# Moving work off GpSimd beside the row gather of a hybrid mLSTM/GLA/PEER block

## The chip, the cores and the metric

The kernel runs on one core of one Trainium2 chip. It has five instruction streams: TensorE (PE, with its weight loads PEld), VectorE (DVE), ScalarE (ACT), GpSimd (POOL) and SyncE (SP, which here only issues DMAs). Each stream runs in its own order, and waits for the others by semaphores. The metric is the time of one execution in microseconds (us). Three runs of the kernel before took 3162.22, 3174.01 and 3175.31 us, so the median is 3174.01 us. The profiled execution took 3167.59 us; its span, from the first to the last instruction, is 3165.8 us, which leaves 1.8 us around it.

## The reference

The layer has two halves. The first, a token mixer with two recurrent head groups, ends before the part that changes here. The second half is PEER, a sparse feed-forward layer with 16,384 experts; each expert is one row u and one row v of 1024 numbers. Per token and head, 16 experts of 16,384 are chosen, and with 8 heads that makes 128 experts for each of the 1024 tokens:

```python
def peer_ffn(h, wq, keys, u_tab, v_tab):
    def retrieve(xb):                               # 128 tokens at a time
        q = (xb @ wq).reshape(PEER_BLOCK, PEER_HEADS, 2, PEER_QDIM // 2)
        s = jnp.einsum('tphq,phkq->tphk', q, keys)
        top_s, top_i = lax.top_k(s, PEER_TOPK)
        ...                                         # best 16 of the 256 pairs: idx, and scores best_s
        g = jax.nn.softmax(best_s.astype(jnp.float32), axis=-1).astype(xb.dtype)
        act = jax.nn.gelu(jnp.einsum('tpkd,td->tpk', u_tab[idx], xb), approximate=False)
        return jnp.einsum('tpk,tpkd->td', g * act, v_tab[idx])
```

So a token's output is the sum over its 128 experts of g * gelu(u . h) * v, in float32.

## The kernel before

The 1024 tokens are eight blocks of 128. Three of them (set A) are computed by gathering, five (set B, 640 tokens) densely.

**The gather.** `gather_all` is a Python generator of some 398 steps, 128 for each block of set A. In step i the queue of GpSimd fetches the u and v rows of one expert per token, 128 rows of 8 KB, into a tile `uv` [128 x 2 x 1024] (L936; four such tiles, and step i fetches for step i + 2). The dot product u . h is one instruction that multiplies and sums (L983 on VectorE). `gate` makes gelu and the factor g on ScalarE (L948, L949), and `add` adds act * v to the block's sum on VectorE (L961). Until the dense stage that sum lies in PSUM (`accP`), afterwards in SBUF (`acc`); `settle` copies it over. While `share[0]` is 2, during query stage B, every other dot product is split: GpSimd multiplies (L981) and ScalarE sums (L947).

**The dense part.** For set B the scores of all 128 x 128 experts are computed: `u_side` multiplies the h of set B by a chunk of 128 u rows (`ua`, 48 matmuls, L1017). Each float32 operand is split into a high and a low part, so that three cheaper products replace one. The high part of u is made on ScalarE (`uh`, L1042), the low part `ul` (L1043) before the dense stage on GpSimd and in it on VectorE. The first 84 chunks are done early (`early_all`), beside the work on queries, and stored in DRAM; the other 44 come in the dense stage, in which the chunks are multiplied by v (`po`, L1405).

**The stages.** Query stage A finds the experts of set A. From 870 us on the gather and the early chunks run beside: selection A (870 to 985 us), query stage B (985 to 1150: projections `pq`, top-16 searches on VectorE, splits `qlo` of the query weights on GpSimd, L1122), selection B (1150 to 1367), and the table loop (1367 to 1829), which builds the gates of set B. One of its 80 iterations makes four one-hot tiles on VectorE (L1294 to L1297, o, oh, ol and oh again) and 16 small matmuls `gb` (L1275, L1276), whose results ScalarE copies out (L1278). What is left of the early chunks follows (1829 to 1866; here called the tail), and then the dense stage to the end.

**What sets the order.** The instructions of every engine stand as the Python code emits them. `ticks` advances the gather by a fixed rate per microsecond of modelled work. `fill` advances the early chunks by quarters (12 matmuls, 1.6 us in its account) as long as the modelled clock of TensorE is behind that of VectorE plus 6 us. When the table loop ends, the quarters that are left are emitted in a row, with 0.2 gather steps per modelled us. The one-hot tiles of the loop have two buffers each, and the `gb` matmuls of an iteration are emitted one iteration later.

## Time and profile before

| what | value |
|---|---|
| median of three runs | 3174.01 us |
| profiled execution | 3167.59 us |
| its span | 3165.8 us |
| mean granted TensorE clock | 0.952 |
| PE, PEld, DVE, ACT, POOL busy over the span | 91%, 81%, 80%, 41%, 31% |
| data moved | 831.44 MB, mean 263 GB/s |

The clock is a share of 2.4 GHz: in a stretch at 1.0 TensorE had its full clock, at 0.5 it had 1.2 GHz. A view of stretches has, for each engine, its busy time in us in that stretch and the number of its instructions, then the granted clock, the mean busy share of the 16 DMA engines and the rate they moved data at. A float32 matmul stands in the trace as two records. A row on one line of the code has the least, the median and the largest duration in ns. A row on waits says who waited for whom, the sum in us, how often, and the longest.

### The profile page before, as it was taken

To read this page: it belongs to the slowest core of one execution; us is meant where nothing else is said; L and a number is where in the kernel's file an instruction comes from. 1 tells how busy PE (TensorE), PEld (TensorE's weight loads), DVE (VectorE), ACT (ScalarE), POOL (GpSimd) and SP (SyncE) were. 2 spreads that over 40 slices of the span, in tenths; PEclk is the share of its full clock that TensorE was granted. 3 is DMA by queue.
4 is the path that set the end of the run, shared out by engine and by line. 5 is a ranking of instruction groups with operands and counts; after the bars stand their busy time and mean duration, and the time that the engine had idled before them with its cause. 6 is when DMAs were issued, how large, how long until landed. Compare 5 with 4: busy or idle time off the path is not lost.

```text
span 3165.8 us, 47649 instructions
## 1 busy us (share of the span) xinstructions
PE 2882.2 (91%) x17321; PEld 2555.5 (81%) x17321; DVE 2518.5 (80%) x4809; ACT 1307.1 (41%) x2909; POOL 973.6 (31%) x760
## 2 busy tenths in 40 slices
PE   7999998998998997878898889999998999999997
PEld 3799896776998987878887888888887788888885
DVE  6633318666798999999999958888888788888885
ACT  4622224444443454545555634333333333333332
POOL 1000002323455776654443432222222222222211
PEclk9999999789999998889999999999999999999999
DMA  5155428535367876768898999999999899999983
GB/s 208 58 181 165 132 85 268 169 107 193 108 231 267 287 269 231 248 225 311 322 317 298 335 349 341 346 342 335 338 345 350 308 332 332 341 337 343 343 292 116
DMA packets 374380, 831.44 MB, mean 263 GB/s; under 512 B 27000, under 2 KB 198648, under 8 KB 324736
## 3 DMA queue, kind: packets, MB, share of 16 engines
q0 software_dynamic: 57600, 411.07, 34.9%
q1 hardware_dynamic: 292624, 347.74, 34.4%
q10 hardware_dynamic: 23920, 69.59, 5.6%
q8 instruction: 136, 2.23, 0.3%
q14 instruction: 100, 0.82, 0.1%
HBM read 729.38 MB, written 98.91 MB: 262 GB/s over the span
## 4 chain that ended last, share of the span: by engine, by line
issue 27%; DVE 17%; POOL 8%; PE 4%; DMA 1%; ACT 0%; POOLq 0%; SPq 0%; DVEq 0%
POOL uv L936 8%; DVE ol L1296 4%; PE po L1405 3%; DVE uv L983 3%; DVE accP L961 2%; DVE oh L1297 2%; DVE oh L1295 2%; DVE o L1294 2%; PE ua L1017 2%; DMA vr<-uv 1%; DMA uv<-uv,idx 1%; DVE acc L961 0%; DVE vl L1371 0%; DVE accB L1412 0%; DMA ft<-d_mod 0%
## 5 line engine op out<-in xcount | busy, mean ns | idle before, releaser
L936 POOL DMA_INDIRECT uv<-uv,idx x384 | 454.5, 1184 | 1299.1 <-DVE acc L961 891.5
L1405 PE MATMUL po<-vh,wh 128*128 128x512 f32 x1255 | 498.8, 397 | 49.7 <-DVE accB L1412 45.4
L1017 PE MATMUL ua<-hBhi,uh 128*128 128x320 f32 x2048 | 492.1, 322 | 39.0 <-ACT uh L1042 26.6
L1405 PE MATMUL po<-vl,wh 128*128 128x512 f32 x1255 | 498.4, 397 | 12.1 <-DVE vl L1371 12.0
L1017 PE MATMUL ua<-hBhi,ul 128*128 128x320 f32 x2048 | 482.5, 318 | 22.0 <-POOL ul L1043 21.7
L1405 PE MATMUL po<-vh,wl 128*128 128x512 f32 x1255 | 495.3, 395 | 0.0
L1017 PE MATMUL ua<-hBlo,uh 128*128 128x320 f32 x2048 | 480.9, 317 | 0.0
L983 DVE SCALAR_TENSOR_TENSOR uv<-uv,h2a 128x1024 f32<-128x1024 f32 x351 | 437.4, 1246 | 49.3 <-DMA uv<-uv,idx 48.9
L1017 PEld LDWEIGHTS ua<-hBhi,uh 128*128 128x128 f32 x2048 | 356.1, 196 | 45.9 <-ACT uh L1042 28.8
L1017 PEld LDWEIGHTS ua<-hBhi,ul 128*128 128x128 f32 x2048 | 355.0, 195 | 26.5 <-POOL ul L1043 26.5
L1017 PEld LDWEIGHTS ua<-hBlo,uh 128*128 128x128 f32 x2048 | 356.9, 195 | 0.0
L1405 PEld LDWEIGHTS po<-vh,wh 128*128 128x128 f32 x1255 | 240.0, 191 | 108.7 <-DVE accB L1412 53.4
L961 DVE SCALAR_TENSOR_TENSOR acc<-uv,act,acc 128x1024 f32<-128x1024 f32 x237 | 303.2, 1279 | 0.2 <-ACT act L949 0.2
L1405 PEld LDWEIGHTS po<-vl,wh 128*128 128x128 f32 x1255 | 240.1, 191 | 65.4 <-DVE vl L1371 17.7
L1405 PEld LDWEIGHTS po<-vh,wl 128*128 128x128 f32 x1255 | 240.3, 191 | 50.5
L1043 POOL TENSOR_TENSOR ul<-ur,uh 128x512 fp32r<-128x512 f32 x170 | 236.6, 1415 | 79.8 <-ACT uh L1042 75.5
L1381 ACT ACTIVATE wh<-w 128x640 fp32r<-128x640 f32 x128 | 94.6, 739 | 396.8 <-DVE w L1378 395.2
L1370 ACT ACTIVATE vh<-vr 128x512 fp32r<-128x512 f32 x251 | 156.6, 625 | 161.3 <-PE po L1405 160.9
L948 ACT ACTIVATE act<-act 128x1 f32<-128x1 f32 x384 | 75.9, 198 | 318.5 <-DVE uv L983 316.7
L961 DVE SCALAR_TENSOR_TENSOR accP<-uv,act,accP 128x1024 f32<-128x1024 f32 x144 | 184.6, 1282 | 15.1 <-ACT act L949 15.1
L1371 DVE TENSOR_TENSOR vl<-vr,vh 128x512 fp32r<-128x512 f32 x251 | 170.9, 685 | 25.3 <-ACT vh L1370 24.8
L1278 ACT ACTIVATE gtl<-gb 128x512 f32<-128x512 f32 x160 | 160.3, 1111 | 71.6 <-PE gb L1276 62.8
(376 smaller groups left out, 5668.7 us busy)
## 6 DMA issues: line engine op xcount, KB each, us to landing
ur<-uC SPq DMA_DIRECT2D x256, 256.0 KB, 6.4
vr<-uv SPq DMA_DIRECT2D x256, 256.0 KB, 7.1
d_G<-gtl ACTq DMA_DIRECT2D x80, 512.0 KB, 5.4
gch<-d_G SPq DMA_DIRECT2D x64, 640.0 KB, 9.7
d_A<-w ACTq DMA_DIRECT2D x84, 320.0 KB, 5.3
w<-d_A SPq DMA_DIRECT2D x84, 320.0 KB, 7.6
wm<-w_mod SPq DMA_DIRECT2D x32, 512.0 KB, 3.9
qraw<-wq SPq DMA_DIRECT2D x32, 512.0 KB, 4.3
```

Of the source, the lines that this page charges most:

```text
L936: G.indirect_dma_start(out=t.rearrange("p a d -> p (a d)"), out_offset=None, in_=A["uv"], in_offset=bass.IndirectOffsetOnAxis(ap=idxs[n][: ...
L948: S.activation(acts[i], acts[i], AF.Gelu)
L961: V.scalar_tensor_tensor(acc, v, act, acc, op0=ALU.mult, op1=ALU.add)
L983: V.scalar_tensor_tensor(t, t, 1.0, h2s[n], op0=ALU.mult, op1=ALU.mult, accum_out=acts[i])
L1017: T.matmul(pt[:, :b - a], l[:, kt], m[:, kt, a:b], start=(kt == 0 and wi == 0), stop=(kt == KT - 1 and wi == 2))
L1043: usplit[0].tensor_tensor(ul[:, k], ur, uh[:, k].bitcast(F32), op=ALU.subtract)
L1278: S.activation(gt[:, :, tt:tt + 4].rearrange("p e t -> p t e"), pt.rearrange("p (t e) -> p t e", e=P), AF.Copy, scale=1.0 / 4096.0)
L1296: V.tensor_tensor(ol, oh, pairs(glT, b, t0), op=ALU.mult)
L1370: S.activation(vh, vr[n], AF.Copy)
L1371: V.tensor_tensor(vl, vr.pop(n), vh.bitcast(F32), op=ALU.subtract)
L1381: S.activation(wh, w, AF.Copy)
L1405: T.matmul(po, st[:, b * P:(b + 1) * P], m, start=(start and wi == 0), stop=(stop and wi == 2))
```

## The change

From the first selection on GpSimd keeps the row fetches alone, up to the end of the dense stage. The lower parts of u (`ul`) and of the query weights of stage B (`qlo`) are made on VectorE, a whole chunk of [128 x 1024] in one instruction, and all dot products are made on VectorE. Of the sums before the dense stage, the even steps stay on VectorE, with the sum in SBUF; the odd ones go to TensorE: ScalarE builds a diagonal matrix `dg` of the 128 factors (L961 of the changed kernel), and two float32 matmuls [128 x 512] multiply it by the v row into PSUM. `settle` adds both sums. The early chunks are loaded in one DMA of 512 KB, with three such tiles where there were six halves. The modelled clocks get other costs: 1.95 or 2.6 us of VectorE per gather step (2.35 or 1.75 before), 0.87 us of TensorE per step, 0.3 us of VectorE per quarter chunk.

```diff
...
     gsA = [ga.tile([P, P], F32, name=f"g{n}") for n in range(ng)]
 
-    accs, psum = {}, []
+    accs, psum, mine, shut = {}, [], {}, [False]
 
     def row(name):
         return gr.tile([P, D], F32, tag="ha", name=name, bufs=3)
 
     def settle(n):
 
-        t = row("acc")
-        for h in range(2):
-            S.activation(t[:, h * 512:h * 512 + 512], accs[n][:, h * 512:h * 512 + 512], AF.Copy)
-        accs[n] = t
+        if n in mine:
+            if not shut[0]:
+                dg = dgp.tile([P, P], F32, tag="dg", name="dg")
+                V.memset(dg, 0.0)
+                for h in range(2):
+                    T.matmul(psum[0][:, h * 512:h * 512 + 512], dg, bc(ident.unsqueeze(1), [P, 4, P]), start=False,
+                             stop=True)
+            V.tensor_tensor(accs[n], accs[n], mine.pop(n), op=ALU.add)
 
     def gather_all():
         total = ng * P
-        uvs, h2s, acts, prods = {}, {}, {}, {}
+        uvs, h2s, acts = {}, {}, {}
 
         def fetch(i):
             n, k = divmod(i, P)
...
 
         def gate(i):
             n, k = divmod(i, P)
-            if i in prods:
-                t = prods.pop(i)
-                S.activation(t, t, AF.Copy, accum_out=acts[i])
             S.activation(acts[i], acts[i], AF.Gelu)
             S.activation(acts[i], acts[i], AF.Copy, scale=gsA[n][:, k:k + 1])
 
         def add(i):
             n, k = divmod(i, P)
             act = acts.pop(i)
-            if k == 0:
-                accs[n] = psum[0] if psum else row("acc")
-            acc = accs[n]
             v = uvs.pop(i)[:, 1]
             if k == 0:
-                V.tensor_scalar(acc, v, act, None, op0=ALU.mult)
+                accs[n] = row("acc")
+                V.tensor_scalar(accs[n], v, act, None, op0=ALU.mult)
+            elif psum and k % 2:
+                dg = dgp.tile([P, P], F32, tag="dg", name="dg")
+                S.activation(dg, ident, AF.Copy, scale=act)
+                fresh = n not in mine
+                mine[n], shut[0] = psum[0], k == P - 1
+                for h in range(2):
+                    c = slice(h * 512, h * 512 + 512)
+                    T.matmul(psum[0][:, c], dg, v[:, c], start=fresh, stop=shut[0])
             else:
-                V.scalar_tensor_tensor(acc, v, act, acc, op0=ALU.mult, op1=ALU.add)
+                V.scalar_tensor_tensor(accs[n], v, act, accs[n], op0=ALU.mult, op1=ALU.add)
 
         fins = []
         start(0)
...
                 n, k = divmod(i, P)
                 t = uvs[i][:, 0]
                 acts[i] = gr.tile([P, 1], F32, tag="act", name="act", bufs=3)
-                if share[0] and i % share[0] == 0:
-                    prods[i] = t
-                    G.tensor_tensor(t, t, h2s[n], op=ALU.mult)
-                else:
-                    V.scalar_tensor_tensor(t, t, 1.0, h2s[n], op0=ALU.mult, op1=ALU.mult, accum_out=acts[i])
+                V.scalar_tensor_tensor(t, t, 1.0, h2s[n], op0=ALU.mult, op1=ALU.mult, accum_out=acts[i])
                 if k == P - 6 and n + 1 < ng:
                     start(n + 1)
             if i:
                 add(i - 1)
                 if i % P == 0:
-                    if psum:
-                        settle(i // P - 1)
+                    settle(i // P - 1)
                     fins.append(finish_steps(oA[i // P - 1], accs[i // P - 1], i == total))
                     next(fins[-1])
             yield
...
     blo = hB.tile([P, KT, nd], F32R, name="hBlo")
     up = es.enter_context(tc.tile_pool(name="up", bufs=2))
     eru = ExitStack()
-    ru = [eru.enter_context(tc.tile_pool(name="ru", bufs=6))]
+    dgp = eru.enter_context(tc.tile_pool(name="dg", bufs=2))
+    ru = [eru.enter_context(tc.tile_pool(name="ru", bufs=3)), KT]
 
     def cuts_of(n):
         return [(0, n)] if n <= 512 else [(0, n // 2), (n // 2, n)]
...
             if kt % 2:
                 yield 2 * 3 * sum(b - a for a, b in cuts) / 2400.0
 
-    us, wr, ubank, ulim, usplit = {}, {}, [bank], [early + 1], [G]
+    us, wr, ubank, ulim = {}, {}, [bank], [early + 1]
 
     first = [c for c in range(P) if (c + 1) * early // P != c * early // P]
     plan = first + [c for c in range(P) if c not in first]
...
     def u_load(c):
         if c < ulim[0] and c not in us:
             us[c] = []
-            for k in (0, 4):
-                ur = ru[0].tile([P, 4, P], F32, tag="ru", name="ur")
-                Y.dma_start(ur, A["uC"][plan[c]][:, k:k + 4])
-                us[c].append(ur)
+            m = ru[1]
+            for k in range(0, KT, m):
+                ur = ru[0].tile([P, m, P], F32, tag="ru", name="ur")
+                Y.dma_start(ur, A["uC"][plan[c]][:, k:k + m])
+                us[c].append((slice(k, k + m), ur))
 
     def u_prep(c):
         if c >= P or isinstance(us[c], tuple):
             return
         uh = up.tile([P, KT, P], F32R, tag="uh", name="uh")
         ul = up.tile([P, KT, P], F32R, tag="ul", name="ul")
-        for n, ur in enumerate(us[c]):
-            k = slice(4 * n, 4 * n + 4)
+        for k, ur in us[c]:
             S.activation(uh[:, k], ur, AF.Copy)
-            usplit[0].tensor_tensor(ul[:, k], ur, uh[:, k].bitcast(F32), op=ALU.subtract)
+            V.tensor_tensor(ul[:, k], ur, uh[:, k].bitcast(F32), op=ALU.subtract)
         us[c] = (uh, ul)
 
     def u_side(c, ahead):
...
             yield from u_side(n, True)
             S.dma_start(d_A[n], wr.pop(c))
 
-    share = [0]
     gather, earlier = gather_all(), early_all()
     steps = [ng * P + 14]
     owed, spare = [0.0], [(early - 4) * KT // 2]
...
             owed[0] -= 1.0
             next(gather, None)
             steps[0] -= 1
-            clock["DVE"] += 2.35 - (1.2 / share[0] if share[0] else 0)
+            clock["DVE"] += 1.95 if psum else 2.6
+            if psum:
+                clock["PE"] += 0.87
 
     def fill():
 
...
                 return
             spare[0] -= 1
             clock["PE"] += next(earlier)
+            clock["DVE"] += 0.3
 
     def dve(us_, rate, more=True):
         clock["DVE"] += us_
...
                     hi = wh.tile([P, KT, P], F32R, tag="qhi", name="qhi")
                     lo = wh.tile([P, KT, P], F32R, tag="qlo", name="qlo")
                     S.activation(hi, raw, AF.Copy)
-                    (G if g else V).tensor_tensor(lo, raw, hi.bitcast(F32), op=ALU.subtract)
+
+                    (G if g and ticking >= 0 else V).tensor_tensor(lo, raw, hi.bitcast(F32), op=ALU.subtract)
                     parts[g] = (hi, lo)
                     load(g + 2)
 
...
             V.tensor_copy(ghT[:, b], t)
             V.tensor_tensor(glT[:, b], t, ghT[:, b], op=ALU.subtract)
 
-        share[0] = 2
         query_stage(oB, bhi, blo, "B", doneB, lambda g: None, lambda: None, -1, True)
-        share[0] = 0
         with tc.tile_pool(name="gbl", bufs=1) as gp:
 
             T2 = TB // 2
...
                 g_store()
 
+    for n in list(mine):
+        settle(n)
     eru.close()
     hB2 = es.enter_context(tc.tile_pool(name="hB2", bufs=1))
     acc = hB2.tile([P, nb, D], F32, name="accB")
-    ru[0] = es.enter_context(tc.tile_pool(name="ru2", bufs=2))
+    ru[:] = es.enter_context(tc.tile_pool(name="ru2", bufs=2)), KT // 2
     ulim[0] = P
-
-    usplit[0] = V
-    for n in list(accs):
-        if accs[n] is psum[0]:
-            settle(n)
     psum.clear()
     esp.close()
     pa = es.enter_context(tc.tile_pool(name="pa", bufs=8 - len(cuts_of(nd)), space=PSUM))
```

Three places show how the order moves. The first is VectorE in the table loop, about an iteration of it. Before:

```order
L1294 TENSOR_TENSOR o_14856<-io,i1T 128x1024
L1295 TENSOR_TENSOR oh<-io,i2T 128x1024
L1296 TENSOR_TENSOR ol<-oh,glT 128x1024
L1297 TENSOR_TENSOR oh<-oh,ghT 128x1024
L983 SCALAR_TENSOR_TENSOR uv,act<-uv,h2a 128x1024
L961 SCALAR_TENSOR_TENSOR accP<-uv,act,accP 128x1024
L1294 TENSOR_TENSOR o_14943<-io,i1T 128x1024
```

And after, at the same place in the program:

```order
L1301 TENSOR_TENSOR oh<-oh,ghT 128x1024
L986 SCALAR_TENSOR_TENSOR uv,act<-uv,h2a 128x1024
L968 SCALAR_TENSOR_TENSOR acc<-uv,act,acc 128x1024
L1298 TENSOR_TENSOR o_14644<-io,i1T 128x1024
L1299 TENSOR_TENSOR oh<-io,i2T 128x1024
L1300 TENSOR_TENSOR ol<-oh,glT 128x1024
L1301 TENSOR_TENSOR oh<-oh,ghT 128x1024
L986 SCALAR_TENSOR_TENSOR uv,act<-uv,h2a 128x1024
L1046 TENSOR_TENSOR ul<-ur,uh 128x1024
```

The sum (`acc`) stands behind every other dot product only, it lies in SBUF, and the split `ul` of a whole chunk has come to stand on VectorE.

The second place is the queue of GpSimd from the start of the table loop on (the iota makes the loop's number row). Before:

```order
L1256 IOTA io 128x256
L936 DMA uv<-uv,idx_7050 128x2048
L1043 TENSOR_TENSOR ul<-ur,uh 128x512 x2
L936 DMA uv<-uv,idx_7050 128x2048
L1043 TENSOR_TENSOR ul<-ur,uh 128x512 x2
L936 DMA uv<-uv,idx_7050 128x2048 x2
```

After:

```order
L1260 IOTA io 128x256
L940 DMA uv<-uv,idx_7050 128x2048 x48
L940 DMA uv<-uv,idx_7051 128x2048 x128
L940 DMA uv<-uv,idx_7052 128x2048 x128
L1446 TENSOR_TENSOR accB<-accB,ft 128x512
```

The fetches, which stood between pairs of splits, now stand alone up to the end of the dense stage.

The third place is TensorE in the table loop, at the end of one iteration's `gb` matmuls and the start of the next quarter of an early chunk. Before:

```order
L1275 MATMUL gb<-o_14983,oh 128x128
L1276 LDWEIGHTS ol
L1276 MATMUL gb<-o_14983,ol 128x128
L1017 MATMUL ua<-hBhi,uh 128x320 x2
L1017 MATMUL ua<-hBlo,uh 128x320 x2
L1017 MATMUL ua<-hBhi,ul 128x320 x2
```

After:

```order
L1279 MATMUL gb<-o_14190,oh 128x128
L1280 LDWEIGHTS ol
L1280 MATMUL gb<-o_14190,ol 128x128
L966 MATMUL accP<-uv,dg 128x512 x2
L1020 MATMUL ua<-hBhi,uh 128x320 x2
L1020 MATMUL ua<-hBlo,uh 128x320 x2
```

The two matmuls on v stand in TensorE's stream behind the `gb` matmuls and ahead of the early chunk, and what follows waits with them for the diagonal.

Counted over the streams, from the first selection to the dense stage: VectorE has 158 dot products (117 before), 80 sums (149 before, with the first of a block), 85 more splits `ul` and 15 more `qlo`; TensorE has 156 more matmuls of [128 x 512] float32: two for each of 77 odd steps, and two in the `settle` at the start of the dense stage, which closes a sum in the middle of a block. Of the early chunks, 3492 of the 4032 `ua` matmuls stand ahead of the last `gb` matmul, where 3792 did, so 540 are left for the tail instead of 240. By the start of the dense stage 158 gather steps are done, where 150 were.

## Rows read from the trace of the kernel before

**Rows 1.** Stretches: busy us (instructions) per engine, clock, DMA share, GB/s.

```profile
870.00:985.00 115.00, 95.48 (x612) 94.15 (x612) 106.06 (x341) 50.83 (x91) 57.83 (x43) 0.90 0.67 236
985.00:1150.00 165.00, 157.14 (x1078) 154.37 (x1079) 156.71 (x694) 77.82 (x196) 119.58 (x72) 0.98 0.80 280
1150.00:1367.00 217.00, 170.82 (x1013) 165.41 (x1012) 213.50 (x545) 107.19 (x220) 141.63 (x92) 0.86 0.70 241
1367.00:1829.00 462.00, 401.87 (x3309) 387.56 (x3308) 454.33 (x517) 263.71 (x457) 191.43 (x148) 0.95 0.87 307
1829.00:1866.00 37.00, 37.00 (x250) 37.00 (x248) 17.46 (x21) 13.86 (x34) 20.06 (x16) 0.95 0.97 378
1866.00:3090.00 1224.00, 1158.96 (x5726) 1001.05 (x5725) 1045.45 (x1443) 423.22 (x1039) 279.25 (x235) 0.98 0.94 334
```

**Rows 2.** Timeline at 1499 us: start, us, engine, line, instruction.

```profile
1499.41 3.25 DVE L1296 TENSOR_TENSOR ol<-oh,glT 128x1024 f16<-128x1024 f16 x1
1499.61 2.50 POOL L1043 TENSOR_TENSOR ul<-ur,uh 128x512 fp32r<-128x512 f32 x2
```

**Rows 3.** VectorE before the dense stage, by line: busy us, mean ns, idle before.

```profile
L983 DVE SCALAR_TENSOR_TENSOR uv<-uv,h2a 128x1024 f32<-128x1024 f32 x114 | 148.8, 1305 | 14.3 <-DMA uv<-uv,idx 14.3
L1296 DVE TENSOR_TENSOR ol<-oh,glT 128x1024 f16<-128x1024 f16 x80 | 128.0, 1601 | 2.8
...
L822 DVE SCALAR_TENSOR_TENSOR t<-row,col 128x128 f32<-128x128 int32 x8 | 5.5, 692 | 0.3
```

**Rows 4.** Five VectorE lines over the whole trace: least, median, largest duration in ns.

```profile
L1296 DVE TENSOR_TENSOR ol<-oh,glT x80: 691/693/3329, 1370.1 to 1827.0; 128x1024 f16<-128x1024 f16 x80
...
L983 DVE SCALAR_TENSOR_TENSOR uv<-uv,h2a x351: 1199/1217/3115, 906.6 to 3076.6; 128x1024 f32<-128x1024 f32 x176
...
L822 DVE SCALAR_TENSOR_TENSOR t<-row,col x8: 291/292/1411, 884.5 to 1336.8; 128x128 f32<-128x128 int32 x8
...
L961 DVE SCALAR_TENSOR_TENSOR accP<-uv,act,accP x144: 1261/1283/1299, 916.7 to 1864.7; 128x1024 f32<-128x1024 f32 x144
...
L1122 DVE TENSOR_TENSOR qlo<-qraw,qhi x2: 1219/1222/1224, 780.1 to 985.6; 128x1024 fp32r<-128x1024 f32 x2
```

**Rows 5.** GpSimd before the dense stage, by line, columns as in rows 3.

```profile
L1043 POOL TENSOR_TENSOR ul<-ur,uh 128x512 fp32r<-128x512 f32 x170 | 236.6, 1415 | 79.8 <-ACT uh L1042 75.5 <-issue 3.5
L936 POOL DMA_INDIRECT uv<-uv,idx x150 | 176.2, 1174 | 380.2 <-DVE accP L961 253.7 <-DVE v L780 37.3 <-DVE best L780 22.0
L981 POOL TENSOR_TENSOR uv<-uv,h2a 128x1024 f32<-128x1024 f32 x33 | 81.6, 2472 | 0.6
L1122 POOL TENSOR_TENSOR qlo<-qraw,qhi 128x1024 fp32r<-128x1024 f32 x15 | 35.9, 2396 | 10.4 <-ACT qhi L1121 8.2 <-ACT act L948 2.3
```

**Rows 6.** TensorE lines in 83.1 to 84.9 us and 1834.9 to 1866 us.

```profile
L248 PE MATMUL al<-Z,w x6: 379/592/592, 82.8 to 84.5; 128*128 128x512 f32 x4, 128*128 128x256 f32 x2
...
L1017 PE MATMUL ua<-hBlo,uh x72: 309/309/309, 1834.8 to 1865.8; 128*128 128x320 f32 x72
```

**Rows 7.** Timeline of TensorE, first and last of 16 matmuls of one table iteration.

```profile
1510.40 0.23 PE L1275 MATMUL gb<-o,oh 128*128 128x128 f16 x1
...
1511.27 0.22 PE L1276 MATMUL gb<-o,ol 128*128 128x128 f16 x1
```

**Rows 8.** Waits before the dense stage: sum us, times, longest us.

```profile
POOL uv L936 <- DVE accP L961: 253.1, 63, 9.0
...
PE gb L1275 <- DVE oh L1297: 47.5, 28, 4.0
...
PE ua L1017 <- POOL ul L1043: 21.7, 11, 4.0
```

**Rows 9.** DMA issues in the table loop: size, count, median us to landing.

```profile
uv<-uv,idx POOLq DMA_INDIRECT x63, 8.1
```

**Rows 10.** Waits of TensorE in the dense stage.

```profile
PE po L1405 <- DVE accB L1412: 45.4, 17, 5.7
```

**Rows 11.** VectorE in the dense stage, by line, columns as in rows 3.

```profile
L983 DVE SCALAR_TENSOR_TENSOR uv<-uv,h2a 128x1024 f32<-128x1024 f32 x237 | 288.7, 1218 | 34.9 <-DMA uv<-uv,idx 34.6
```

## The prediction

> **What bounds the kernel now.** I read the stretches first [rows 1]. In the dense stage TensorE is busy for 1159 of 1224 us at a clock of 0.98, and the change leaves that stage's own instructions as they are. Between 870 and 1866 us, where the change acts, the picture is another one. VectorE is busy for 157 of 165 us in query stage B, 213.5 of 217 in selection B and 454 of 462 in the table loop; TensorE has 171 of 217 and 402 of 462 in the last two, and its granted clock falls to 0.86 in selection B, so that part of its busy time is at the lower level of 1.2 GHz. VectorE is the bound there, and TensorE waits for its one-hot tiles, 47.5 us in 28 waits [rows 8].
>
> Then I asked what VectorE does with its time. The timeline at 1499 us [rows 2] shows the one-hot product of L1296 lasting 3.25 us while two splits of GpSimd ran, 2.50 us together. The same instruction has a median of 693 ns [rows 4], and a mean of 1601 [rows 3]. So GpSimd holds VectorE up. The size of it: busy time less count times median is 128.0 - 80 x 0.693 = 72.6 us for L1296, 148.8 - 114 x 1.217 = 10.1 for L983, 5.5 - 8 x 0.292 = 3.2 for L822. Done so for all thirteen groups of that view with a longer mean than their usual length, of which L983 is the first and L822 the last [rows 3, 4], it makes 173 us: some 14 in selection A, 4 in query stage B, 57 in selection B and 98 in the table loop. GpSimd's own work in that time is 354 us of arithmetic (L1043, L981, L1122) and 176 us of fetches [rows 5].
>
> The Trainium skill's page "SBUF — State Buffer", section "Who interferes with whom", has the rule for this: a VectorE instruction with two SBUF inputs contends with a GpSimd instruction that reads SBUF, as an exclusive lock, and the later one waits. By that rule the PSUM sum of L961, with one SBUF tensor, should never stretch, and the trace agrees: its largest duration is 1299 ns against a median of 1283 [rows 4].
>
> **The change, part by part.** Removed from VectorE: the 173 us above, if the arithmetic on GpSimd is its whole cause, and 69 sums at 1.28 us, 88 us. Added: 41 dot products (33 that were GpSimd's, and 8 of gather steps that come earlier) at 1.22 plus a readout of 0.08; 85 splits `ul` and 15 `qlo`, all of [128 x 1024], at the 1.222 us that VectorE takes for this shape in L1122 [rows 4]; and two `settle` additions at about 1.28. Added on TensorE: 156 float32 matmuls of [128 x 512]. The four records of this shape in the 83 us stretch start some 0.43 us apart (83.23 to 84.52 us) [rows 6], so two records make a matmul of 0.86 us, and 156 of them 134 us. On ScalarE 77 diagonals replace 33 sums of about 1.06 us; it is busy for 264 of 462 us in the table loop [rows 1], which hides it. If that cover is gone the diagonal's delay is TensorE's, which is the second-last rival below.
>
> I take TensorE's old work by start-to-start spacing, since busy time contains the drain: 72 of one of the three `ua` products start in 31.0 us [rows 6], so 0.146 us for each; 16 `gb` matmuls start in 0.87 us [rows 7], 0.056 each with the last.
>
> Stage by stage, from the old length:
> - Selection A, 115 us. VectorE 106.1 - 14 + 13 splits (15.9) - 5 sums (6.4) = 101.6; TensorE 612 x 0.146 + 10 x 0.86 = 98. With the old idle time of 9 us: 110, so -5.
> - Query stage B, 165 us. VectorE 156.7 - 4 + 15 `qlo` (18.3) + 18 dot products (23.4) - 18 sums (23.1) + 3 `ul` (3.7) = 175. Little of this stage's work was stretched, since its top-16 searches read one operand, so it gets longer: 178, +13.
> - Selection B, 217 us. VectorE 213.5 - 57 + 20 `ul` (24.4) + 15 dot products (19.5) - 15 sums (19.2) = 181, and idle 4: 185, -32.
> - Table loop, 462 us. VectorE 454.3 - 98 + 37 `ul` (45.2) - 30 sums (38.5) = 363. TensorE: 1716 `ua` (2400 less the tail's 684, with the dense stage's first) x 0.146 + 1280 x 0.056 + 62 x 0.86 = 251 + 72 + 53 = 376, so it becomes the longer of the two. The third candidate is the DMA: 307 GB/s in 462 us [rows 1] are 142 MB; six chunks fewer, with 0.52 MB read and 0.33 MB written each, leave 137 MB. At the dense stage's 334 GB/s that lasts 410 us, at the tail's 378 it lasts 362 [rows 1]. I take 410, the rate held for over a thousand microseconds: -52.
> - Tail, 37 us. 540 `ua` x 0.146 + 14 odd-step matmuls of the gather and 2 of `settle` at 0.86 = 93, with VectorE's 56 us beside it: +56. This is work moved out of the loop, and it must be paid.
>
> The sum is -20 us. In the dense stage eight gather steps fewer are left of about 234, so VectorE has some 20 us less to do, but it was not the bound. It holds TensorE up for 45.4 us at the ends of groups [rows 10]; 8/234 of that is 1.6 us. The other end is the DMA: 8 MB at 334 GB/s are 24 us, were it the bound; TensorE's busy 1159 of 1224 says it is not. I take -3, near the first. Below nothing I see no end here, since no instruction is added to that stage.
>
> So the profiled execution's 3167.6 us less 23 is about 3145 us. That execution was 6 us faster than the median of the runs shown, 3174; I don't add it, because 3162 was measured as well.
>
> The unknown in the sum is how well two engines with the same load keep step. TensorE's work from 870 us to the last `gb` matmul is 3492 x 0.146 + 768 projections of the same form + 72 + 140 x 0.86 and some 21 of scores and transposes, 835 us; VectorE's is 821. I ask for 883. In the dense stage TensorE lost 65 of 1224 us by waits, 5%, the same share as here. A share of 1% would give a loop with the DMA at its fast end, one of 9% would eat the gain.
>
> **The rivals.**
> - *The engines keep step, and the DMA follows.* The table loop then ends with TensorE at 378 us, -84 instead of -52, and the dense stage gets back 8 us more, a third of the 24: 3105 us. For it: the one-hot tiles are two deep and the `gb` matmuls an iteration late, so each engine has an iteration (5 us) of play. Against it: a DMA share of 0.87 already [rows 1].
> - *TensorE replaces VectorE, and nothing is won.* It would run at the table loop's mean clock of 0.95 with the old waits for tiles: 835 / 0.95 + 47.5 = 926 us, 43 us more than I ask for: 3188. Half of those waits gives 3164. For it: the odd sums are moved to the engine that has 91% of the span. Against it: the waits came from stretched VectorE instructions, and GpSimd's lateness for `ul` (21.7 us) [rows 8] goes as well.
> - *The slower side: the odd step stalls TensorE's stream.* Its matmul stands ahead of early chunks that could run, and waits for dot product, gelu, scale and diagonal in a row. If each of 77 such matmuls waits as long as one of the 28 waits for tiles, 1.7 us [rows 8], that is 131 us; taken at half, since the next fetch and the step before hide part, 65 us: 3210. It decides from 0.3 us per odd step on (23 / 77), where the gain is gone. Against it: the step's dot product is emitted one gather step earlier, some 6 us in the loop (462 us for 77 to 80 steps).
> - *GpSimd's fetches and VectorE hold each other too, so the 173 us stay.* Then VectorE needs 821 + 173 us to the end of the loop, 994 against the 883 asked for: 3256. Against it: in the dense stage, where GpSimd has fetches alone, L983 has a mean of 1218 ns in 237 executions [rows 11], its undisturbed length. The fp16 tiles are not made in that stage, so it isn't excluded.
>
> The same page of the Trainium skill has a box on the "DVE blocks DMA" trap that speaks against the change from this side: VectorE in a mode that takes both ports keeps GpSimd from writing a fetch's descriptors. It names the opposite direction of that last rival, and here the trace shows fetches that lasted 1174 ns in the mean beside all the work [rows 5] and landed 8.1 us after issue in the loop [rows 9]; how much of the 1174 ns is such a wait, no row shows.
>
> **How the numbers follow.** Chances: forecast (3125 to 3165) 0.52; engines in step 0.15; nothing won (3160 to 3190) 0.17; stalled stream 0.11; fetches still hold VectorE 0.05. The predicted time is the likeliest's, 3145. The range goes down to 3100 for the second case and up to 3190 for the third; 0.15 or so is left outside, nearly all above. About 0.5%, 16 us, is what a measurement of this kernel tells from no change, so "faster" is below 3158: 0.44 of the forecast's 0.52, all of the second case and 0.02 of the third, 0.61. "Slower" is above 3190: 0.02 of the third, 0.09 of the stalled stream and the last case, 0.16. The rest is 0.23.
>
> **What would show it.** L1296 at 0.69 us in the mean, and VectorE's other stretched lines at their medians, shows the removed hold. The records of the odd matmuls start 0.43 us apart if their price is right. The last `gb` matmul should come near 1753 us, the tail should last about 93 us with TensorE full, and query stage B should be longer than 165 us. Waits of TensorE for ScalarE's diagonal above 25 us in all would mean the stalled stream; the mean clock from 870 us on should rise above 0.95. The prediction is wrong if the stretched durations stay, or if the dense stage begins at 1866 us or later although they go.

## The result and the profile after

The changed kernel took 3334.11 us (median of four runs, 3323.16 to 3343.23), the kernel before 3170.27 on the same chip. The ratio is 1.0517, with an interval of 1.0486 to 1.0548: slower by 5.2%, where 3145 us and a small gain had been forecast. The profiled execution of after took 3323.16 us, with a span of 3321.4 us and a mean granted clock of 0.956.

The stretches of after, with the columns of [rows 1] and cut at the same events (selection A, query stage B, selection B, table loop, tail, dense stage) with one row more for the end:

```profile
870.00:994.00 124.00, 102.92 (x632) 95.85 (x632) 98.36 (x348) 51.34 (x82) 17.09 (x16) 0.93 0.64 230
994.00:1203.00 209.00, 180.20 (x982) 152.89 (x982) 159.31 (x671) 56.17 (x155) 30.08 (x31) 0.90 0.57 197
1203.00:1440.00 237.00, 210.62 (x1218) 186.10 (x1218) 194.27 (x638) 101.22 (x202) 42.35 (x36) 0.95 0.66 234
1440.00:1951.00 511.00, 426.43 (x3167) 367.01 (x3166) 367.14 (x524) 257.59 (x430) 81.92 (x65) 0.93 0.75 270
1951.00:2036.00 85.00, 82.47 (x514) 76.19 (x514) 35.59 (x43) 28.49 (x65) 13.90 (x13) 1.00 0.83 302
2036.00:3240.00 1204.00, 1159.12 (x5774) 1001.79 (x5773) 1027.12 (x1418) 420.95 (x1025) 267.08 (x227) 0.99 0.93 333
3240.00:3322.00 82.00, 59.96 (x241) 46.13 (x239) 47.23 (x97) 19.34 (x45) 13.11 (x10) 0.89 0.32 115
```

All of the loss lies between 870 and 2036 us. Every stage there except the tail is longer than forecast, and in the table loop no engine is full: VectorE works for 367 of 511 us (454 of 462 before), TensorE for 426, and the DMA share has fallen from 0.87 to 0.75. A stage without a full engine is a stage of waits.

VectorE, first: the line that GpSimd had stretched (three durations: least, median, largest), and the lines before the dense stage.

```profile
L1300 DVE TENSOR_TENSOR ol<-oh,glT x80: 691/691/694, 1441.7 to 1944.3; 128x1024 f16<-128x1024 f16 x80
```

```profile
L986 DVE SCALAR_TENSOR_TENSOR uv<-uv,h2a 128x1024 f32<-128x1024 f32 x154 | 186.3, 1214 | 2.0 <-DMA uv<-uv,idx 2.0
L1046 DVE TENSOR_TENSOR ul<-ur,uh 128x1024 fp32r<-128x1024 f32 x84 | 102.6, 1222 | 145.3 <-ACT uh L1045 145.2
...
L1298 DVE TENSOR_TENSOR o<-io,i1T 128x1024 f16<-128x1024 f16 x80 | 54.9, 687 | 89.8 <-PE gb L1280 88.1 <-POOL io L1260 1.7
```

In [rows 4] this product (L1296 there) reached 3329 ns; now its largest duration is 694. Dot product and split last what was forecast, 1214 and 1222 ns. What is new is the idle time in front of the split (145.3 us) and of the one-hot tile `o` (89.8 us); in front of the dot product it is 2.0 us. The waits of TensorE and VectorE from 870 to 2060 us (sum, times, longest):

```profile
PE accP L966 <- ACT dg L961: 147.3, 60, 8.2
PE pq L1020 <- ACT qhi L1126: 8.2, 1, 8.2
PE accP L966 <- ACT act L950: 4.8, 2, 2.4
```

```profile
DVE ul L1046 <- ACT uh L1045: 150.4, 48, 8.7
DVE o L1298 <- PE gb L1280: 88.1, 22, 7.6
DVE acc L968 <- ACT act L950: 32.3, 15, 2.4
```

The first row is the odd sum's matmul waiting for its diagonal: 147.3 us in 60 waits. A single one of them, on VectorE, ScalarE and TensorE (start, duration, engine, line, instruction, idle time before it):

```profile
1705.48 0.08 DVE L986 DVE_READ_ACCUMULATOR uv<-uv,h2a 128x1 f32 x1
```

```profile
1707.90 1.93 ACT L1282 ACTIVATE gtl<-gb 128x512 f32<-128x512 f32 x2 [0.66 <-PE gb L1280]
1709.62 0.21 ACT L949 ACTIVATE act<-act 128x1 f32<-128x1 f32 x1
1709.88 0.29 ACT L950 ACTIVATE act<-act,g 128x1 f32<-128x1 f32 x1
1710.21 0.40 ACT L961 ACTIVATE dg<-ident,act 128x128 f32<-128x128 f32 x1
```

```profile
1708.10 0.22 PE L1280 MATMUL gb<-o,ol 128*128 128x128 f16 x1
1710.66 3.46 PE L966 MATMUL accP<-uv,dg 128*128 128x512 f32 x4 [2.34 <-ACT dg L961]
```

On TensorE the odd matmul stands right behind the last `gb` matmul. On ScalarE the gelu, its scaling and the diagonal stand right behind the two copies of that `gb` result. So TensorE finishes `gb` at 1708.32, then ScalarE copies, makes the factor and the diagonal, done at 1710.61, and TensorE goes on at 1710.66. That is a round trip through another engine, 2.34 us long, although the step's dot product had been read out on VectorE by 1705.56, some 4 us before its gelu began.

### The profile page after: what moved, and what is told of

Its sections match the earlier page's. It is cut to its first block, busy times and chain, and to the rows that moved or that the text cites. A ratio compares the mean times of both kernels' runs of the same rounds, so it can differ in the third digit from the quotient of the medians.

```text
span 3321.4 us, 47759 instructions
## 1 busy us (share of the span) xinstructions
PE 3025.6 (91%) x17633; PEld 2598.0 (78%) x17633; DVE 2411.9 (73%) x4901; ACT 1287.8 (39%) x2831; POOL 615.3 (19%) x542
## 4 chain that ended last, share of the span: by engine, by line
issue 29%; PE 25%; POOL 8%; ACT 6%; DVE 3%; DMA 2%; ACTq 0%; POOLq 0%; SPq 0%; DVEq 0%
PE ua L1020 11%; POOL uv L940 8%; PE accP L966 5%; PE pq L1020 4%; PE po L1406 3%; ACT gtl L1282 2%; DMA uv<-uv,idx 1%; PE gb L1279 1%; PE gb L1280 1%; ACT dg L961 1%; ACT act L950 1%; ACT uh L1045 1%; PE sc L1153 1%; ACT w L1061 0%; DVE uv L986 0%
## 5 line engine op out<-in xcount | busy, mean ns | idle before, releaser
L1020 PE MATMUL ua<-hBhi,uh 128*128 128x320 f32 x2048 | 505.4, 328 | 4.5 <-ACT w L1061 1.6
L986 DVE SCALAR_TENSOR_TENSOR uv<-uv,h2a 128x1024 f32<-128x1024 f32 x384 | 466.6, 1217 | 28.9 <-DMA uv<-uv,idx 27.4
L1020 PE MATMUL ua<-hBhi,ul 128*128 128x320 f32 x2048 | 468.7, 310 | 2.6 <-DVE ul L1046 2.6
L1020 PE MATMUL ua<-hBlo,uh 128*128 128x320 f32 x2048 | 469.6, 311 | 0.0
L968 DVE SCALAR_TENSOR_TENSOR acc<-uv,act,acc 128x1024 f32<-128x1024 f32 x304 | 389.1, 1280 | 36.7 <-ACT act L950 36.6
L1020 PEld LDWEIGHTS ua<-hBlo,uh 128*128 128x128 f32 x2048 | 346.1, 190 | 0.0
L966 PE MATMUL accP<-uv,dg 128*128 128x512 f32 x308 | 197.6, 776 | 152.2 <-ACT dg L961 147.3
L1046 DVE TENSOR_TENSOR ul<-ur,uh 128x1024 fp32r<-128x1024 f32 (+1 forms) x171 | 159.2, 951 | 152.7 <-ACT uh L1045 152.6
L966 PEld LDWEIGHTS accP<-uv,dg 128*128 128x128 f32 x308 | 64.2, 229 | 216.1 <-ACT dg L961 160.7
L1061 ACT ACTIVATE w<-ua 128x320 f32<-128x320 f32 x256 | 97.5, 433 | 297.8 <-PE ua L1020 293.3
```

The lines of the kernel that those rows point to most:

```text
L966: T.matmul(psum[0][:, c], dg, v[:, c], start=fresh, stop=shut[0])
L968: V.scalar_tensor_tensor(accs[n], v, act, accs[n], op0=ALU.mult, op1=ALU.add)
L986: V.scalar_tensor_tensor(t, t, 1.0, h2s[n], op0=ALU.mult, op1=ALU.mult, accum_out=acts[i])
L1020: T.matmul(pt[:, :b - a], l[:, kt], m[:, kt, a:b], start=(kt == 0 and wi == 0), stop=(kt == KT - 1 and wi == 2))
L1046: V.tensor_tensor(ul[:, k], ur, uh[:, k].bitcast(F32), op=ALU.subtract)
L1061: S.activation(w[:, a:b], pt[:, :b - a], AF.Gelu)
```

## Experiments

Theory A (latency) says that the odd matmul stalls TensorE's stream while its diagonal is made, and that the other waits follow from it. Theory B (load) says that the added work on TensorE, the float32 matmuls with their weight loads, is too much. Each text below was written before its run. Ratios are to the kernel before, with their intervals.

**A constant in place of the diagonal.** The matmul reads the identity, which is always there. Everything else, the diagonal's making too, stays.

```diff
-T.matmul(psum[0][:, c], dg, v[:, c], start=fresh, stop=shut[0])
+T.matmul(psum[0][:, c], ident, v[:, c], start=fresh, stop=shut[0])
```

> The odd steps' matmuls on TensorE take the constant identity in place of the diagonal of the step's factors, so they don't wait for ScalarE's chain (gelu, scale, diagonal); ScalarE still makes the diagonals, and TensorE has the same number of matmuls. The factor of the odd steps is left out of the sums. Theory A, the chain's latency: TensorE stands idle in front of each odd matmul because the diagonal is queued on ScalarE behind copies of results that TensorE has only just made; this idle time (147 us in the trace after) and the lower clock behind it go, so about 3150 us (3120 to 3180). Theory B, the load: 156 float32 matmuls, 134 us, are simply too much for TensorE in this part, and the waits are only where the lack of time shows; then it stays above 3270 us.

It took 3147.33 us, ratio 0.9927 (0.99 to 0.9955). The load on TensorE is the same (308 records and 308 weight loads on the odd steps, as in the changed kernel), the wait is not, and the whole loss is gone. The table loop:

```profile
1377.00:1785.00 408.00, 398.46 (x3182) 357.33 (x3181) 366.47 (x524) 261.00 (x433) 77.04 (x65) 0.99 0.90 337
```

It lasts 408 us for 511, with the same number of instructions within a per cent, at a clock of 0.99 for 0.93. Theory B falls.

**Two other places in the stream.** The diagonal stays, and the matmul is put on a list (`due`) and issued later: once at the end of the stretch of TensorE work that follows the gather step, once at the start of the next gather step. The diff is the second's; the first has one more `flush()` behind the stretch.

```diff
-for h in range(2):
-    T.matmul(psum[0][:, c], dg, v[:, c], start=fresh, stop=shut[0])
+due.append((dg, v, fresh, shut[0]))
...
 for i in range(total + 1):
+    flush()
```

> The same arithmetic as the changed kernel; the two matmuls of an odd step are emitted behind the quarters of an early chunk that follow the gather step, so TensorE has other work while ScalarE makes the diagonal. 59 of the 76 or so then stand behind early-chunk matmuls, 16 in query stage B still right behind a projection. Theory A: the loop's and the selections' stalls go, those of query stage B (33 us) partly stay: about 3175 us (3145 to 3205). Theory B: no change of more than 30 us from 3334.

> The same arithmetic; the two matmuls of an odd step are emitted at the start of the next gather step, a whole step later, when the diagonal has long been made. The tile of the row is held a step longer, so the next fetch into it is later. Theory A: all stalls go, query stage B's too: about 3160 us (3130 to 3190). Theory B: over 3300 us. A third possibility, C, that the four row tiles are too few: VectorE's waits for fetched rows rise above 60 us and the time lies between.

After the stretch: 3212.04 us, 1.0128 (1.0097 to 1.0158). One step later: 3158.58 us, 0.9973 (0.9951 to 0.9995). The second came as expected; the first missed its range by 7 us, since it cures the loop but does nothing for query stage B (209 us, as after the change), where some of the stall had been expected to go. Its rows for these two:

```profile
1004.00:1213.00 209.00, 182.75 (x977) 154.50 (x978) 159.51 (x671) 56.00 (x154) 30.37 (x31) 0.88 0.57 198
1438.00:1855.00 417.00, 397.85 (x3169) 355.85 (x3168) 367.65 (x524) 259.35 (x431) 80.65 (x64) 0.99 0.90 329
```

The second cures both. Its stages from selection A to the tail, and TensorE's wait for the diagonal over all of them:

```profile
878.00:999.00 121.00, 103.28 (x633) 97.04 (x634) 98.50 (x349) 51.61 (x82) 17.92 (x16) 0.94 0.64 234
999.00:1160.00 161.00, 159.16 (x976) 142.97 (x977) 151.57 (x647) 56.80 (x153) 33.02 (x30) 0.98 0.72 245
1160.00:1377.00 217.00, 204.62 (x1225) 183.93 (x1224) 199.01 (x663) 101.55 (x202) 43.38 (x37) 0.98 0.75 265
1377.00:1787.00 410.00, 395.15 (x3166) 353.97 (x3165) 367.56 (x524) 257.65 (x431) 78.52 (x64) 0.99 0.92 334
1787.00:1872.00 85.00, 85.00 (x528) 78.28 (x527) 35.69 (x43) 28.20 (x66) 16.96 (x14) 1.00 0.84 317
```

```profile
PE accP L928 <- ACT dg L971: 23.3, 9, 6.3
```

147.3 us in 60 waits have become 23.3 in 9, and the loop lasts 410 us. VectorE's wait for the `gb` matmuls ahead of its one-hot tile goes with them, from 88.1 us to 7.1, so it followed from the stall. Beside the identity this is the second sign for theory A, with the computation whole.

**Which half of the change loses.** Once all sums stay on VectorE and only GpSimd's work moves; once TensorE takes the odd sums and GpSimd keeps splits and dot products.

```diff
-elif psum and k % 2:
+elif False:
...
-            clock["DVE"] += 1.95 if psum else 2.6
-            if psum:
-                clock["PE"] += 0.87
+            clock["DVE"] += 2.6
```

```diff
-V.tensor_tensor(ul[:, k], ur, uh[:, k].bitcast(F32), op=ALU.subtract)
+(G if psum else V).tensor_tensor(ul[:, k], ur, uh[:, k].bitcast(F32), op=ALU.subtract)
...
-(G if g and ticking >= 0 else V).tensor_tensor(lo, raw, hi.bitcast(F32), op=ALU.subtract)
+(G if g else V).tensor_tensor(lo, raw, hi.bitcast(F32), op=ALU.subtract)
...
+        if share[0] and i % share[0] == 0:
+            G.tensor_tensor(t, t, h2s[n], op=ALU.mult)
...
```

> The first half of the change alone: GpSimd only fetches, VectorE makes all splits and dot products, and also all sums, in SBUF; nothing of the gather on TensorE or in PSUM. The account of work has 2.6 us of VectorE per step and none of TensorE. VectorE then has some 821 + 87 = 908 us from 870 us to the last table matmul, against 959 us of the kernel before, and 192 early matmuls are left for the tail: about 3130 us (3105 to 3160) by theories A and B alike, since both put the loss on TensorE's part. If it is over 3190 us, the loss lies in the moved splits, and both theories fall.

> The second half of the change alone: the odd sums go to TensorE, emitted as in the changed kernel, while GpSimd keeps the splits ul and qlo and every other dot product of query stage B and selection B, as before. Theory A, the latency of ScalarE's chain in front of each odd matmul: the stalls stay whatever GpSimd does, and GpSimd's hold of VectorE (173 us in the kernel before) comes back on top, so no less than 3334 us, about 3380 (3330 to 3430). Theory D, that the moved splits make VectorE late and with it the dot products on which the diagonals wait: the stalls shrink and it falls below 3280 us.

The second half alone: 3358.93 us, 1.0598 (1.0564 to 1.0632), as theory A expected, with TensorE's wait for the diagonal again:

```profile
PE accP L969 <- ACT dg L964: 163.9, 60, 6.6
```

So the loss belongs to the odd sums, without any help of the moved splits. The first half alone: 3190.46 us, 1.008 (1.0051 to 1.0109), where 3130 had been expected. That is a miss, half a microsecond beyond the bound at which both theories were to fall. Taken by its size it does not fell them: this half loses some 20 us, where the whole change loses 164 and the second half alone 190. But the moved work brings no gain. Its rows from the first early matmul to the loop, and from the loop's first one-hot tile to its last `gb` matmul, with TensorE's wait for the tiles in the loop:

```profile
879.00:1452.00 573.00, 544.05 (x3666) 539.25 (x3667) 518.25 (x1713) 230.21 (x461) 118.19 (x84) 0.98 0.70 250
1452.00:1859.00 407.00, 282.68 (x2401) 267.48 (x2400) 386.98 (x541) 225.27 (x358) 77.48 (x63) 0.75 0.87 309
```

```profile
PE gb L1277 <- DVE oh L1299: 121.2, 44, 5.5
```

The loop is 55 us shorter than before (462), and VectorE sets its pace, busy for 387 of 407 us; TensorE, at a clock of 0.75, waits for it. The loss lies ahead of the loop, in 573 us where the kernel before took 497: VectorE has 42 us more to do there (518 for 476) and TensorE 121 (544 for 423), as 2772 `ua` matmuls stand ahead of the first table matmul, against 1800 before. Up to the last `gb` matmul VectorE is busy for 905 us, near the 908 expected; but the 959 us that these were held against are the length of that stretch before, in which VectorE worked for 931. So only 26 us of its work are gone, because some 150 us of moved splits and dot products (the prediction's terms) stand against the 173 us of holds, and its idle time rises from 28 to 75 us. I put the early matmuls' place down to the raised cost in the modelled clock, and tried it next.

**The account put back.** The same with a step cost of 1.95 until the loop and 2.6 from there, and then also with `ul` made by a function of its own, `u_low`, a quarter chunk later than `uh`.

```diff
-clock["DVE"] += 1.95 if psum else 2.6
+clock["DVE"] += tick_cost[0]
```

```diff
 if ahead and n == 1:
+    u_low(c + 1)
     u_load(c + (3 if c + 1 < early else 2))
```

> As e4_vector_sums (the first half alone, all sums on VectorE), with the account of a gather step put back to 1.95 us until the table loop begins, so fewer early quarters are emitted beside query stage B and the selections: 2292 early matmuls stand ahead of the first table matmul, where e4 had 2772 and the kernels before and after some 1800. If e4 lost its time because TensorE was the bound in selection B (228 us busy of 235) and then idle in the loop (375 of 511, clock 0.79), the last table matmul comes some 50 us earlier and the time is about 3140 us (3120 to 3165). If VectorE's moved splits are the loss by themselves, it stays at 3180 or above.

> As e10_vector_sums_account, with the split ul of the next chunk emitted a quarter of a chunk behind its high part uh instead of right behind it. In e10 VectorE waited 49 us for ScalarE's uh, in whose queue the copies of TensorE's last results stand ahead; before the change it was GpSimd that waited there. If this wait is what the moved splits cost, VectorE wins some 40 us to the last table matmul: about 3145 us (3130 to 3165). If VectorE's plain work is the cost, it stays at 3175 or above.

The first text takes selection B for 1184 to 1419 us and the loop for 1419 to 1930 us (228 of 235, 375 of 511, clock 0.79). But the loop of that kernel lasts from 1452 to 1859 us, as the rows above show; the 511 us hold the end of selection B and the tail as well.

3179.61 us, 1.003 (1.0012 to 1.0049), and 3201.16 us, 1.0093 (1.007 to 1.0115): both missed. 2292 `ua` matmuls still stand ahead of the loop in the first. By the second text's own sign (3175 or above) it is VectorE's work that costs. The later split changes who waits: VectorE's wait for `uh` falls from 49.0 to 30.2 us, and TensorE's for `ul` rises from 18.9 us to 40.1:

```profile
PE ua L1020 <- DVE ul L1052: 40.1, 20, 6.9
```

So the rows show why the first half alone brings no gain: little of VectorE's work is gone, its waits have grown, and more of both engines' work stands ahead of the loop. How much each part costs, no run separates.

**Which share of the odd sums.** With the matmul one step later and `ul` a quarter later: every third (`k % 3 == 1`) and every fourth (`k % 4 == 3`) step on TensorE, with the modelled costs scaled.

```diff
-elif psum and k % 2:
+elif psum and k % 3 == 1:
```

> As e3_next_step, with every third step's sum on TensorE instead of every other, the account of work changed to fit (2.17 and 0.58 us per step), and the split ul emitted a quarter of a chunk later than uh, so VectorE doesn't wait for ScalarE's copy. By the work: TensorE 849 us and VectorE 854 us to the last table matmul, which comes near 1785 us, with 192 early matmuls in the tail instead of 540 and 149 gather steps done instead of 158: 58 us won by the dense stage's start, some 16 given back in it, so about 3117 us (3095 to 3145). If waits rather than work set e3's time, it stays at 3150 or above.

> As e7_every_third, with every fourth step on TensorE (2.28 and 0.43 us per step in the account). VectorE has 16 us more, TensorE 22 us less: VectorE is the bound, about 3125 us (3100 to 3155).

3163.82 us, 0.9977 (0.9958 to 0.9997), and 3183.65 us, 1.0053 (1.0031 to 1.0075). Both were expected near 3120 and missed: taking load off TensorE won nothing here, and by the first text's own sign (3150 or above) waits rather than work set the time. The likewise later `ul` with every other step:

> As e3_next_step (odd matmuls a gather step later), with ul a quarter of a chunk behind uh. In e3 VectorE waited 81 us for uh, but TensorE is busy 395 of 410 us in the loop there, at a clock of 0.99, and the DMA share is 0.92, so little is to be had: 3152 us (3140 to 3162). If VectorE's waits set the pace in e3, 3125 us or below.

3159.85 us, 0.9964 (0.9947 to 0.998), as expected, and no different from the kernel without it (0.9973). Beside this one, every third step does win 55 us between the last `gb` matmul and the first `po` matmul (64 us for 119), as the smaller tail was to give. It gives back 26 us ahead of the loop, where 2028 `ua` matmuls stand instead of 1776, 5 in the loop, and 26 in the dense stage.

**The queue position on ScalarE.** The changed kernel with one difference: ScalarE's two copies of `gb` are issued behind the gelu and the diagonal of the next step, not ahead of them. A1 puts the stall on that position, A2 on the chain of gelu, scale and diagonal itself.

```diff
         ticks(us_, rate)
+        copies[0]()
...
-                    S.activation(gt[:, :, tt:tt + 4].rearrange("p e t -> p t e"),
-                                 pt.rearrange("p (t e) -> p t e", e=P), AF.Copy, scale=1.0 / 4096.0)
+                    held.append((gt[:, :, tt:tt + 4].rearrange("p e t -> p t e"),
+                                 pt.rearrange("p (t e) -> p t e", e=P)))
...
+            def copy_out():
+                while held:
+                    S.activation(*held.pop(0), AF.Copy, scale=1.0 / 4096.0)
```

> The changed kernel with one difference, on ScalarE's queue in the table loop: the two copies of a table iteration's results (gtl) are emitted behind the next gather step's gelu, scale and diagonal instead of ahead of them. TensorE's and VectorE's orders are as in the changed kernel, with the odd matmuls still right behind the gb matmuls. Theory A1, the diagonal is late because it is queued behind copies that wait for matmuls TensorE has only just made: in the loop the idle time in front of the odd matmuls (88 us in 32 steps) goes, with some 25 us of low clock; the stalls of the selections and of query stage B stay: about 3220 us (3190 to 3250). Theory A2, the chain itself (dot product, gelu, scale, diagonal, 0.9 us on ScalarE alone) is too long wherever it is queued: over 3290 us.

3271.26 us, 1.0332 (1.0299 to 1.0365), between the two ranges, so neither text held. TensorE's wait for the diagonal in the loop (84.6 us in 32 waits after the change) becomes

```profile
PE accP L966 <- ACT dg L961: 34.4, 28, 5.2
```

and the loop goes from 511 to 445 us. So the place behind the copies is somewhat over half of the loop's stall; the rest is put down to the chain itself, which no run takes apart.

**More steps before the dense stage.** The kernel with the later matmul, and the tail's gather rate doubled (`sige` 0.2 to 0.4).

> As e3_next_step, with 0.4 gather steps per modelled us in the tail in place of 0.2, so 172 steps stand ahead of the dense stage instead of 158. If a gather step costs the dense stage 1.8 us, as the stage lengths of the kernels before and after say (1264 and 1249 us with 150 and 158 steps done), the dense stage gets 25 us shorter and the tail by 7 odd steps, 12 us, longer: 3146 us. If a step costs the dense stage 0.4 us, as the prediction had it (3 us for 8), the sum is a loss: 3166 us.

3172.1 us, 1.0007 (0.999 to 1.0025): nothing won, and nearer the second sum (3166) than the first. With 172 steps done instead of 158 the dense stage (first `po` matmul to the end) falls from 1245 to 1235 us, but from the last `gb` to the first `po` matmul it takes 145 us instead of 121. So 14 steps more took 0.7 us each off the dense stage, and cost more than that ahead of it. VectorE waits there for the fetched rows (43.4 us in 22 waits), while the DMA is full:

```profile
1787.00:1885.00 98.00, 94.10 (x537) 80.59 (x535) 56.36 (x71) 34.92 (x93) 30.01 (x25) 1.00 0.98 386
```

## Why the prediction was wrong

**The step that failed** is the one on the diagonals: "On ScalarE 77 diagonals replace 33 sums ..., which hides it." ScalarE's busy share, 264 of 462 us, was taken as the cover. But a share of busy time says nothing on where an instruction stands. ScalarE had time; it did the diagonal late, in an order that made TensorE wait for a result of its own last instruction. The stalled stream was among the rivals with the right mechanism, but its price, half of a 1.7 us wait per step or 65 us, was taken from waits for one-hot tiles (measured: 150 us for 70 steps, 2.1 us each), and "emitted one gather step earlier" was said against it. That holds for the dot product; gelu, scale and diagonal are emitted in the step itself.

What it cost: the last `gb` matmul came at 1951 us instead of 1753, 198 us late. Ahead of it stand 70 of the odd pairs. In front of these TensorE was idle for 150 us, and for 9 in the kernel with the identity, 141 us more. The pairs themselves, from the start of the first record to that of the last, take 131 us, and 95 with the identity, since 34 of them ran at the lower clock level at least in part (3 with the identity): 36 us more. From the first early matmul to the last `gb` matmul the kernel with the identity takes 903 us for 1081, 178 less; 141 and 36 make 177, though TensorE's other idle time went the other way (12 us, and 33 with the identity), so the agreement is closer than the parts. The other 20 of the 198 are in the kernel with the identity too, 903 us where 883 were forecast.

```profile
L966 PE MATMUL accP<-uv,dg x308: 590/697/1223, 925.7 to 2041.3; 128*128 128x512 f32 x154
```

```profile
L966 PE MATMUL accP<-uv,ident x308: 590/592/1222, 933.8 to 1871.4; 128*128 128x512 f32 x154
```

These two rows are the odd matmuls of after and of the kernel with the identity: the same count, a median of 697 ns and of 592, which is the full-speed duration of this shape in [rows 6].

Step by step:
- *GpSimd's hold goes:* right. The 173 us are down to 3.7 (the same sum over the same groups). This agrees with the lock that the Trainium skill describes in "SBUF — State Buffer", section "Who interferes with whom": none of GpSimd's arithmetic on SBUF is left there, and VectorE's product lasts 691 to 694 ns. The rival that fetches hold VectorE too is refuted by the same rows, and with GpSimd's splits back the sum is 142 us.
- *VectorE's own work:* right, 367 us in the loop (363 forecast) and 819 up to the last `gb` matmul (821).
- *The matmul's price:* right at the full clock, 0.43 us between records; at the lower level it is twice that, which the sum had left out.
- *The loop by the DMA, 410 us at 334 GB/s:* wrong as it stood (511), and 410 us at 334 GB/s once the stall is taken away (the kernel with the matmul one step later). That it fits so closely is partly luck: the reason given for it, the DMA's rate, isn't shown, since TensorE is busy for 395 of the 410 us there too. *The tail:* 85 us, 93 forecast, in both.
- *Selections and query stage B:* 124, 209 and 237 us, where 110, 178 and 185 were forecast. Without the stall 121, 161 and 217, still 26 more in sum. What the forecast had left out there: GpSimd's wait for ScalarE's `uh` (75.5 us in [rows 5]) comes over to VectorE with the splits. It is 150.4 us after the change, and 80.8 without the stall:

```profile
DVE ul L1055 <- ACT uh L1054: 80.8, 45, 6.4
```

- *The dense stage, -3 us:* mis-sized. From the first `po` matmul to the end it took 1264 us before and 1249 after, -15, and that is with 8 gather steps fewer. The other kernels of 158 steps have 1240 to 1252 us, those of 149 have 1266 to 1278. So eight or nine steps less went with some 2 us each, not with a share of TensorE's waits [rows 10]; but 14 more brought only 0.7 us each, and what sets this price stays open. The waits did fall, from 45.4 to 34.5 us:

```profile
PE po L1406 <- DVE accB L1413: 34.5, 14, 8.2
```

- *The mean clock from 870 us on should rise above 0.95:* taken to the end it is 0.96, as it was before, so the sign as worded tells nothing. Up to the last `gb` matmul it is 0.93, as before; with the matmul one step later it is 0.98.
- *The signs named in advance:* a wait for the diagonal above 25 us was to show the stalled stream (147.3), and a dense stage from 1866 us on although the holds go was to show the prediction wrong (2072).

What stays open: which part of the moved work makes the kernels with all sums on VectorE 0.3 to 0.9% slower than before, and where the early matmuls would have to stand for a smaller share on TensorE to pay. With the stall gone the DMA's share in the loop is 0.90 to 0.92 at 324 to 337 GB/s, so the DMA may be what is reached next; no run tested it.

The best two versions are the change with the odd matmul issued one gather step later, with and without the later split: 0.9964 (0.9947 to 0.998) and 0.9973 (0.9951 to 0.9995). Even the identity, with no wait for a diagonal at all, gives only 0.9927. So the change had some 0.3% in it, and the place of the odd matmul in the instruction stream cost 5.5%.

## What to carry to other kernels

When a part of a sum moves to another engine, follow each operand through the programs of all the engines that make it, and see what stands directly ahead of it there: if that is a consumer of the receiving engine's latest result, the move is a round trip, whatever the busy shares say. Issue such a consumer one step later than its producer; a list of two lines did it here. And when an instruction moves to another engine, its waits can move with it, as the one for `uh` did here, so add them to the new engine's sum; hold its work against the old work there, not against the old length.

## What was not expected of the hardware

The lower clock came with the stalls: where TensorE stopped for 2.5 us in the mean at 60 of the odd steps, its granted clock was 0.90 to 0.95, and with the same instructions and few stops 0.98 to 0.99 from query stage B to the loop's end. Of the odd pairs 34 of 78 ran at the lower level at least in part in the one case, and 4 in the other. So the stalls cost TensorE more than their length: 36 us here beside 141, against the kernel with the identity.

GpSimd's fetches lasted as long without its arithmetic as with it: the mean of the 157 fetches before the dense stage is 1165 ns, where [rows 5] has 1174.
